# Latent attention on one core: full-row product of the query's high and the key's low part, query loads ahead of the key products, half of the key copies on GpSimd

## The chip, the cores and the metric

The kernel runs on one core of one Trainium2 chip. A core has five engines with a queue of instructions each: TensorE (PE, the matmuls; the profile shows its weight loads apart as PEld), VectorE (DVE), ScalarE (ACT), GpSimd (POOL) and SyncE (SP, which here issues nearly all DMAs). Each engine works through its queue in order, and semaphores tie the queues together. Matmul operands lie in SBUF with up to 128 rows (partitions), results go to PSUM. The metric is the device time of one execution in microseconds (us), lower is better.

## The reference: what is computed

The program is a two-layer trunk on 1024 tokens of width 1024, in float32: layer 0 mixes by a state-space scan and a convolution, layer 1 by a sparse attention and a latent attention, and each layer ends with an output product and a gated side input. The change lies in the latent attention of layer 1 alone:

```python
def mla_mixer(c_q, c_kv, k_rope, positions, q_norm, kv_norm, w_uq, w_ukv):
    q = (rms_norm(c_q, q_norm) @ w_uq).reshape(bsz, s_len, MLA_HEADS, MLA_NOPE + MLA_ROPE)     # 8 heads, 64 + 32
    kv = (rms_norm(c_kv, kv_norm) @ w_ukv).reshape(bsz, s_len, MLA_HEADS, MLA_NOPE + MLA_V)
    q = jnp.concatenate([q[..., :MLA_NOPE], rope(q[..., MLA_NOPE:], positions)], axis=-1)
    k_r = jnp.broadcast_to(rope(k_rope[:, :, None, :], positions), (bsz, s_len, MLA_HEADS, MLA_ROPE))
    k = jnp.concatenate([kv[..., :MLA_NOPE], k_r], axis=-1)
    v = kv[..., MLA_NOPE:]
    ...
    def one_block(i):                                                                          # 128 queries
        qb = lax.dynamic_slice_in_dim(q, t0, Q_BLOCK, axis=1)
        s = jnp.einsum('bqhd,bkhd->bhqk', qb, k).astype(f32) * scale
        mask = kpos[None] <= (t0 + jnp.arange(Q_BLOCK))[:, None]
        return jnp.einsum('bhqk,bkhd->bqhd', masked_softmax(s, mask), v)
```

## The kernel before

**Precision.** A product of two float32 matrices is made from split operands: a high part (rounded to the matmul's format) and a low part (the rest), as hi*hi + hi*lo + lo*hi. For a score, the 64 non-rotary features of one head are laid out so that one 128-row matmul carries two of these terms: query tile `QA` holds for each head the high part in one half of the rows and the low part in the other, key tile `KA` holds the key's high part in both halves. The third term, query high by key low, is a matmul of its own: it takes the 64 rows of `QA` with the high part, `QA[pr, h4]`, and 64 rows of `KB` with the key's low part (`KB` holds two heads, one in rows 0 to 63 and one in rows 64 to 127). The rotary features with all three terms are stacked on 96 rows (`QR`, `KR`).

**Order of the stage.** `layer1` runs the sparse attention `nsa`, then `mla_keys(0)`, then `mla`. `mla_keys(u)` makes the keys and values of four heads (u is 0 or 1): two products into PSUM (L1474), whose high part ACT writes to `kh` (L1476, in `parts` L107) and whose low part DVE writes to `KB` (L108); then eight DMAs from `kh` fill `KA` (L1479), four of which move 64 rows to other rows and four of which leave the rows as they are; then eight products of 128 tokens give the values `vm` (L1484, L1485). `mla` allots `qmslot`, makes POOL touch it behind `KA` (L1492), loads `KR` (L1493) and goes through 16 steps: u = 0 with eight blocks of 128 queries, then u = 1. A step loads `QA` and `QR` (L1501, L1502) into one of three places of `qmslot`, and the gate (L1504); then for each head the scores against n = 128 (i + 1) keys in pieces of at most 512 columns: `QA` by `KA` (L1518), on the last piece the causal mask as a bfloat16 matmul (L1263), `QA[pr]` by `KB` (L1521), `QR` by `KR` (L1522). DVE takes the row maximum (L1234), ACT the exponentials (L1237), DVE scales (L1246), PE transposes (L1258), ACT copies the transposes to SBUF (L1259), PE multiplies by the values (L1530), and `store_y` writes the result. Score tiles have two PSUM buffers of two banks. After step 3 `mla_keys(1)` runs.

**What sets the order.** Tiles and queues are planned by a scheduler that runs ahead of time: it keeps program order as priority, may put a ready instruction ahead of one that isn't, and fixes each engine's queue. `t16` tiles (16 KB a partition) share nine places; when `mla` begins, four of them hold the layer's output and five are given back by the sparse attention as its last reads end.

The sparse attention (`nsa`) has the same softmax and two score matmuls for each piece, L1333 with 128 rows and L1338 with 112.

Of the kernel before, what the change touches and what calls it, by code (L numbers as in the profile page):

```python
# [6 lines left out]
F32 = mybir.dt.float32  # L7
F32R = mybir.dt.float32r
# [14 lines left out]
class Trunk:  # L23
# [1441 lines left out]
    def mla_keys(self, u):  # L1465

        nc = self.nc
        if u == 0:
            self.KAm = []
            self.KBm, self.vm = self.t16([2, 2, 1024], F32R, name="KBm"), self.t16([2, 8, 256], name="vm")  # L1470
        KA, KB, vm = self.t16([4, 1024], F32R, name="KAm"), self.KBm[:, u], self.vm[:, u]
        Ck = [(self.Ck[:, 0], self.Ck[:, 1])]
        for q in range(2):
            ps = self.up(self.wk, 256 * u + 128 * q, Ck)  # L1474
            hi = self.t4((1024,), F32R, name="kh")
            self.parts(hi, KB[:, q], ps, nc.vector)  # L1476
            for b in range(2):
                for half in (0, 64):
                    nc.sync.dma_start(KA[half:half + 64, 2 * q + b].bitcast(F32), hi[64 * b:64 * b + 64].bitcast(F32))  # L1479
        vs = slice(512 + 256 * u, 768 + 256 * u)  # L1480
        for i in range(8):
            ts = slice(128 * i, 128 * i + 128)
# [4 lines left out]

    def mla(self):
        nc = self.nc
        Qs = self.t16([4, 2, 4, 128], F32R, name="qmslot")  # L1490
        KR = Qs[0:96, 3].rearrange("p a h t -> p (a h t)")
        self.after(KR[:, 0:1], self.KAm[0][0:96, 0, 0:1])  # L1492
        nc.sync.dma_start(KR.bitcast(F32), self.kr_dram.bitcast(F32))  # L1493
        for step in range(16):
            u, i = divmod(step, 8)
            ts = slice(128 * i, 128 * i + 128)
            nk, n = i + 1, 128 * (i + 1)
            hs = slice(4 * u, 4 * u + 4)
            KA, KB, vm = self.KAm[u], self.KBm[:, u], self.vm[:, u]
            QA, QR = Qs[:, step % 3, 0], Qs[0:96, step % 3, 1]  # L1500
            nc.sync.dma_start(QA.bitcast(F32), self.qm_dram[hs, :, ts].rearrange("h p t -> p h t").bitcast(F32))  # L1501
            nc.sync.dma_start(QR.bitcast(F32), self.qr_dram[hs, :, ts].rearrange("h p t -> p h t").bitcast(F32))  # L1502
# [5 lines left out]
            for s0 in range(0, 4, hg):  # L1508
                S = self.bank2().rearrange("p (h n) -> p h n", h=hg)
                for s_ in range(hg):  # L1510
                    b, q = divmod(s0 + s_, 2)
                    h4 = 2 * q + b
                    pr = slice(64 * b, 64 * b + 64)
                    for c in range(0, n, 512):
# [6 lines left out]
                        nc.tensor.matmul(o_, QA[pr, h4], KB[pr, q, ks], start=False, stop=False)  # L1521
# [16 lines left out]
    def layer1(self):  # L1538
# [30 lines left out]
        self.run(nsa)  # L1569
        self.mla_keys(0)  # L1570
# [70 lines left out]
```

## Time and profile before

| | |
|---|---|
| median of 3 runs | 1639.42 us (1637.12 to 1641.62) |
| profiled execution | 1643.63 us, of it span 1641.8 us |
| PE busy | 1522.7 us, 93% of the span, 8284 matmuls |
| DVE, ACT, POOL busy | 1004.4 (61%), 636.3 (39%), 360.4 us (22%) |
| chain that ended last | PE 72%, DVE 17%, DMA 3% |
| mean granted TensorE clock | 0.955 of full speed |
| latent attention in the span | from about 1211 us (first key product) to about 1428 us |

The profile is of one execution. A matmul's busy time is modelled with its drain, so neighbours overlap: what a matmul costs in a stream is the distance from its start to the start of the next one, which the text calls its pitch. The granted clock of 1.00 is 2.4 GHz, 0.50 is 1.2 GHz. "X <- Y" in a wait means that X sat idle until Y.

### The profile page before, as it was taken

The numbers are of one execution on the slowest core, as the hardware profiler recorded it, in microseconds if no ns is written. First come the engines' busy times: TensorE is split into PE (matmuls) and PEld (weight loads), VectorE is DVE, ScalarE is ACT, GpSimd is POOL, SyncE is SP. The second block draws the span as 40 slices with busy tenths as digits, with TensorE's granted clock in tenths as the row PEclk, the third lists the DMA queues.
The fourth block names the chain that finished last, engine by engine and source line by source line (L and its number), as shares of the span: only waits on it lengthen the run. The fifth ranks groups of instructions, "written<-read, shape, count | busy, mean of one in ns | idle before, by whom it ended". The sixth has DMA issues, their size and how long they took to land.

```text
span 1641.8 us, 22311 instructions
## 1 busy us (share of the span) xinstructions
PE 1522.7 (93%) x8284; PEld 1193.1 (73%) x8284; DVE 1004.4 (61%) x2248; ACT 636.3 (39%) x1297; POOL 360.4 (22%) x319
## 2 busy tenths in 40 slices
PE   4799899779998999799998979999999999999998
PEld 4697787667786888698876756666666676777787
DVE  6899999778435554751586246777744566444411
ACT  5332122166213333322342127777654565412210
POOL 4528633421225002312222200000000000132400
PEclk8899999889999999899999979999996999999999
DMA  8012453413424324242722264120043230422421
GB/s 244 14 52 79 139 180 111 146 52 129 157 78 142 128 87 135 82 143 85 180 90 90 77 193 125 54 67 22 27 98 85 66 92 25 143 95 94 151 87 68
DMA packets 140380, 168.65 MB, mean 103 GB/s; under 512 B 19432, under 2 KB 107232, under 8 KB 140272
## 3 DMA queue, kind: packets, MB, share of 16 engines
q1 hardware_dynamic: 135568, 155.82, 30.8%
q0 software_dynamic: 4544, 11.38, 2.3%
q8 instruction: 66, 1.08, 0.3%
q14 instruction: 42, 0.34, 0.1%
q10 hardware_dynamic: 160, 0.01, 0.0%
HBM read 112.10 MB, written 50.99 MB: 99 GB/s over the span
## 4 chain that ended last, share of the span: by engine, by line
PE 72%; DVE 17%; DMA 3%; ACT 2%; issue 2%; SPq 2%; POOL 1%; ACTq 0%; DVEq 0%; POOLq 0%
PE S L114 39%; PE tr L1258 7%; DVE conv L264 5%; PE o L1353 5%; PE tr L114 3%; PE o L1530 3%; PE S L1338 2%; PE S L1521 2%; PE S L1522 2%; PE S L1333 2%; PE S L1518 1%; PE tr L802 1%; PE S L1263 1%; SPq L1294 1%; PE tr L973 1%
## 5 line engine op out<-in xcount | busy, mean ns | idle before, releaser
L114 PE MATMUL S<-xT,wt 128*128 128x512 f32 x768 | 188.3, 401 | 4.3 <-DVE ext L249 4.3
L1234 DVE TENSOR_REDUCE nm<-S 128x1 f32<-128x640 f32 (+7 forms) x132 | 129.4, 981 | 101.8 <-PE S L1522 65.1
L114 PE MATMUL S<-X,wt 128*128 128x512 f32 x768 | 184.6, 396 | 5.8 <-ACT wt L107 2.3
L114 PE MATMUL S<-wo,Y 128*128 128x512 f32 x768 | 181.4, 395 | 5.0 <-DVE gb L688 3.6
L114 PE MATMUL S<-wg,hT 128*128 128x512 f32 x720 | 176.8, 403 | 9.5 <-ACT wg L107 4.0
L114 PEld LDWEIGHTS S<-xT,wt 128*128 128x128 f32 x768 | 144.9, 192 | 35.8 <-DVE ext L249 5.1
L114 PEld LDWEIGHTS S<-X,wt 128*128 128x128 f32 x768 | 143.1, 190 | 37.0 <-issue 4.0
L114 PEld LDWEIGHTS S<-wo,Y 128*128 128x128 f32 x768 | 143.8, 189 | 35.7 <-DVE gb L688 3.9
L114 PEld LDWEIGHTS S<-wg,hT 128*128 128x128 f32 x720 | 136.7, 193 | 42.2 <-ACT wg L107 7.3
L264 DVE SCALAR_TENSOR_TENSOR conv<-ext,conv 128x1024 f32<-128x1024 f32 x116 | 148.9, 1284 | 2.3
L108 POOL TENSOR_TENSOR wt<-raw,wt 128x1024 fp32r<-128x1024 f32 x34 | 82.8, 2451 | 115.9 <-ACT wt L107 115.8
L1237 ACT ACTIVATE pslot<-S,nm 128x640 f32<-128x640 f32 (+7 forms) x128 | 89.9, 709 | 25.6 <-DVE nm L1234 14.6
L1259 ACT COPY PT<-tr 128x512 f32<-128x512 f32 (+3 forms) x172 | 80.2, 492 | 46.5 <-PE tr L1258 42.3
L1258 PE MATMUL tr<-ident,pslot 128*128 128x128 f32 x528 | 84.7, 284 | 0.0
L1353 PE MATMUL o<-PT,vslot 128*64 128x256 f32 x528 | 84.5, 391 | 0.0
L1258 PEld LDWEIGHTS tr<-ident,pslot 128*128 128x128 f32 x528 | 58.7, 142 | 29.8 <-issue 20.8
L97 DVE TENSOR_SCALAR rs_v<-ss 128x1 f32<-128x1 f32 x32 | 4.9, 153 | 119.4 <-ACT lh L93 99.1
L1338 PE MATMUL S<-kst,qslot 112*128 112x512 f32 (+3 forms) x192 | 74.4, 400 | 0.0
L1333 PE MATMUL S<-kst,qslot 128*128 128x512 f32 (+3 forms) x192 | 70.3, 366 | 2.3 <-ACT pslot L1237 1.4
L787 POOL TENSOR_TENSOR lh<-lh 128x1024 f32<-128x1024 f32 x16 | 39.9, 2496 | 120.1 <-DVE lh L786 96.5
L852 DVE SCALAR_TENSOR_TENSOR ov<-ov,S 128x1024 f32<-128x1024 f32 (+1 forms) x17 | 19.7, 1157 | 73.3 <-issue 44.7
L93 ACT ACTIVATE lh<-S 128x1024 f32<-128x1024 f32 x16 | 16.4, 1028 | 123.3 <-issue 94.8
(433 smaller groups left out, 2858.8 us busy)
## 6 DMA issues: line engine op xcount, KB each, us to landing
h_dram<-lh POOLq DMA_DIRECT2D x16, 512.0 KB, 3.2
hr<-h_dram SPq DMA_DIRECT2D x14, 512.0 KB, 3.4
raw<-ev_w_in SPq DMA_DIRECT2D x16, 256.0 KB, 4.3
raw<-ev_w_in SPq DMA_DIRECT2D x8, 512.0 KB, 6.9
raw<-ev_w_out SPq DMA_DIRECT2D x8, 512.0 KB, 4.4
t<-ple_gate SPq DMA_DIRECT2D x8, 512.0 KB, 5.9
raw<-ple_gate SPq DMA_DIRECT2D x8, 512.0 KB, 6.3
lh<-x SPq DMA_DIRECT2D x8, 512.0 KB, 3.9
```

Source lines behind the costliest of these rows:

```text
L108: (eng or self.nc.gpsimd).tensor_tensor(lo, raw, hi, OP.subtract)
L114: self.nc.tensor.matmul(ps, l, r, start=n == 0, stop=n == len(seq) - 1)
L264: nc.vector.scalar_tensor_tensor(out=last if s == 30 else acc, in0=src, scalar=wc, in1=acc, op0=OP.mult, op1=OP.add)
L787: nc.gpsimd.tensor_tensor(hv, hv, xr, OP.add)
L1234: nc.vector.tensor_reduce(out=nm[:, 0:hg], in_=S[:, :, 0:n], op=OP.max, axis=AX.X, negate=True)
L1237: nc.scalar.activation(out=P[:, h, 0:n], in_=S[:, h, 0:n], func=AF.Exp, bias=nm[:, h:h + 1], accum_out=sm[:, h:h + 1])
L1258: nc.tensor.transpose(ps[:, c:c + 128], P[:, h, 128 * (k0 + k):128 * (k0 + k) + 128], self.ident)
L1259: nc.scalar.copy(PT[:, k0:k0 + n, s0:s0 + hg], ps[:, 0:128 * n * hg].rearrange("p (k h t) -> p k h t", h=hg, t=128))
L1333: nc.tensor.matmul(o_, QA[:, hd], KA[:, y, ks], start=True, stop=False)
L1338: nc.tensor.matmul(o_, qb[:, hd], KB[:, y, ks], start=False, stop=True)
L1353: nc.tensor.matmul(o[64 * y:64 * y + 64].rearrange("p g t -> p (g t)"), self.vsw[:, k0 + kt, 128 * br + 64 * y:128 * br + 64 * y + 64], PT ...
L1530: nc.tensor.matmul(o[64 * b:64 * b + 64, q], vm[:, kt, vs], PT[:, kt, 2 * b + q], start=(kt == 0), stop=(kt == nk - 1))
```

## The change

The query tile `qmslot` is allotted in a new function `mla_begin`, which `layer1` calls ahead of `mla_keys(0)`; there POOL zeroes two blocks of it and SP loads `KR` and the queries of steps 0 and 1. A step's queries now have two places in turn and not three, and a third query block `QB` takes, in two DMAs of 64 rows, the high parts alone, with zeros in the other 64 rows; the product with `KB` is then over all 128 rows. The loads of steps 2 to 15 stay at the head of their step. In `mla_keys`, the four copies to `KA` that keep their rows are made by POOL, the other four stay DMAs of SP. `KA` is allotted ahead of `KB` and `vm`.

```diff
--- before.py
+++ after.py
@@ -1465,10 +1465,11 @@
     def mla_keys(self, u):
 
         nc = self.nc
+        KA = self.t16([4, 1024], F32R, name="KAm")
         if u == 0:
             self.KAm = []
             self.KBm, self.vm = self.t16([2, 2, 1024], F32R, name="KBm"), self.t16([2, 8, 256], name="vm")
-        KA, KB, vm = self.t16([4, 1024], F32R, name="KAm"), self.KBm[:, u], self.vm[:, u]
+        KB, vm = self.KBm[:, u], self.vm[:, u]
         Ck = [(self.Ck[:, 0], self.Ck[:, 1])]
         for q in range(2):
             ps = self.up(self.wk, 256 * u + 128 * q, Ck)
@@ -1476,7 +1477,11 @@
             self.parts(hi, KB[:, q], ps, nc.vector)
             for b in range(2):
                 for half in (0, 64):
-                    nc.sync.dma_start(KA[half:half + 64, 2 * q + b].bitcast(F32), hi[64 * b:64 * b + 64].bitcast(F32))
+                    dst, src = KA[half:half + 64, 2 * q + b], hi[64 * b:64 * b + 64]
+                    if half == 64 * b:
+                        nc.gpsimd.tensor_copy(dst, src)
+                    else:
+                        nc.sync.dma_start(dst.bitcast(F32), src.bitcast(F32))
         vs = slice(512 + 256 * u, 768 + 256 * u)
         for i in range(8):
             ts = slice(128 * i, 128 * i + 128)
@@ -1485,21 +1490,42 @@
             nc.scalar.copy(vm[:, i], ps)
         self.KAm.append(KA)
 
+    def mla_begin(self):
+
+        nc = self.nc
+        Qs = self.Qm = self.t16([8, 4, 128], F32R, name="qmslot")
+        KR = self.KRm = Qs[0:96, 6:8].rearrange("p a h t -> p (a h t)")
+        for a in range(2):
+
+            nc.gpsimd.memset(Qs[:, 4 + a].bitcast(F32), 0.0)
+        self.mla_load(0)
+        nc.sync.dma_start(KR.bitcast(F32), self.kr_dram.bitcast(F32))
+        self.mla_load(1)
+
+    def mla_load(self, step):
+        nc, Qs = self.nc, self.Qm
+        u, i = divmod(step, 8)
+        ts, hs = slice(128 * i, 128 * i + 128), slice(4 * u, 4 * u + 4)
+        QA, QB, QR = Qs[:, step % 2], Qs[:, 4 + step % 2], Qs[0:96, 2 + step % 2]
+        nc.sync.dma_start(QA.bitcast(F32), self.qm_dram[hs, :, ts].rearrange("h p t -> p h t").bitcast(F32))
+        for b in range(2):
+            pr = slice(64 * b, 64 * b + 64)
+            nc.sync.dma_start(QB[pr, b:4:2].bitcast(F32),
+                              self.qm_dram[4 * u + b:4 * u + 4:2, pr, ts].rearrange("h p t -> p h t").bitcast(F32))
+        nc.sync.dma_start(QR.bitcast(F32), self.qr_dram[hs, :, ts].rearrange("h p t -> p h t").bitcast(F32))
+
     def mla(self):
         nc = self.nc
-        Qs = self.t16([4, 2, 4, 128], F32R, name="qmslot")
-        KR = Qs[0:96, 3].rearrange("p a h t -> p (a h t)")
-        self.after(KR[:, 0:1], self.KAm[0][0:96, 0, 0:1])
-        nc.sync.dma_start(KR.bitcast(F32), self.kr_dram.bitcast(F32))
+        Qs, KR = self.Qm, self.KRm
         for step in range(16):
             u, i = divmod(step, 8)
             ts = slice(128 * i, 128 * i + 128)
             nk, n = i + 1, 128 * (i + 1)
             hs = slice(4 * u, 4 * u + 4)
             KA, KB, vm = self.KAm[u], self.KBm[:, u], self.vm[:, u]
-            QA, QR = Qs[:, step % 3, 0], Qs[0:96, step % 3, 1]
-            nc.sync.dma_start(QA.bitcast(F32), self.qm_dram[hs, :, ts].rearrange("h p t -> p h t").bitcast(F32))
-            nc.sync.dma_start(QR.bitcast(F32), self.qr_dram[hs, :, ts].rearrange("h p t -> p h t").bitcast(F32))
+            QA, QB, QR = Qs[:, step % 2], Qs[:, 4 + step % 2], Qs[0:96, 2 + step % 2]
+            if step >= 2:
+                self.mla_load(step)
             sgm = self.t2([2, 128], name="sgm")
             nc.sync.dma_start(sgm, self.gm_dram[2 * u:2 * u + 2, :, ts].rearrange("g p t -> p g t"))
             hg = self.group_size(n)
@@ -1510,7 +1536,6 @@
                 for s_ in range(hg):
                     b, q = divmod(s0 + s_, 2)
                     h4 = 2 * q + b
-                    pr = slice(64 * b, 64 * b + 64)
                     for c in range(0, n, 512):
                         m = min(512, n - c)
                         ks = slice(c, c + m)
@@ -1518,7 +1543,7 @@
                         nc.tensor.matmul(o_, QA[:, h4], KA[:, h4, ks], start=True, stop=False)
                         if c + m == n:
                             self.add_mask(S[:, s_, n - 128:n], self.mask_diag)
-                        nc.tensor.matmul(o_, QA[pr, h4], KB[pr, q, ks], start=False, stop=False)
+                        nc.tensor.matmul(o_, QB[:, h4], KB[:, q, ks], start=False, stop=False)
                         nc.tensor.matmul(o_, QR[:, h4], KR[:, ks], start=False, stop=True)
                 P = self.t4(name="P").rearrange("p (h n) -> p h n", h=hg)
                 self.softmax_group(S, n, None, P)
@@ -1567,6 +1592,7 @@
         next(nsa)
         self.run(mq)
         self.run(nsa)
+        self.mla_begin()
         self.mla_keys(0)
         self.mla()
         self.Wo.append(self.out_weights(1, 1, self.w16))
```

## Rows read from the trace of the kernel before

**Rows 1.** Waits from 1262 to 1428 us: who waited for whom, us in total, times, longest.

```profile
DVE nm L1234 <- PE S L1522: 40.9, 35, 2.3
```

**Rows 2.** Busy time by stretch: us, engines busy (instructions), granted clock, DMA share, GB/s.

```profile
1180.00:1200.00 20.00, 20.00 (x143) 13.63 (x143) 15.46 (x33) 14.35 (x32) 0.00 (x0) 1.00 0.01 2
1228.00:1262.00 34.00, 34.00 (x115) 22.15 (x116) 11.64 (x30) 12.17 (x40) 0.00 (x0) 0.51 0.32 85
1262.00:1428.00 166.00, 166.00 (x1184) 116.14 (x1182) 95.49 (x203) 93.74 (x209) 8.03 (x6) 1.00 0.29 82
1510.00:1524.00 14.00, 9.96 (x37) 6.28 (x35) 8.69 (x16) 5.86 (x8) 6.09 (x5) 0.88 0.23 76
```

**Rows 3.** PE in order of time, one head with 768 keys: start, us, instruction.

```profile
1293.43 0.48 PE L1518 MATMUL S<-KAm,qmslot 128*128 128x512 f32 x1
1293.85 0.50 PE L1521 MATMUL S<-KBm,qmslot 64*128 64x512 f32 x1
1294.27 0.50 PE L1522 MATMUL S<-qmslot 96*128 96x512 f32 x1
1294.61 0.28 PE L1518 MATMUL S<-KAm,qmslot 128*128 128x256 f32 x1
1294.74 0.23 PE L1263 MATMUL S<-mbf 128*128 128x128 bf16 x1
1294.90 0.38 PE L1521 MATMUL S<-KBm,qmslot 64*128 64x256 f32 x1
1295.21 0.39 PE L1522 MATMUL S<-qmslot 96*128 96x256 f32 x1
1295.43 0.40 PE L1518 MATMUL S<-KAm,qmslot 128*128 128x512 f32 x1
```

**Rows 4.** PE in order of time, scores of the sparse attention, 512 columns.

```profile
1207.29 0.40 PE L1333 MATMUL S<-kst,qslot 128*128 128x512 f32 x1
1207.53 0.23 PE L1263 MATMUL S<-mbf 128*128 128x128 bf16 x1
1207.57 0.48 PE L1338 MATMUL S<-kst,qslot 112*128 112x512 f32 x1
1207.89 0.38 PE L1258 MATMUL tr<-ident,pslot 128*128 128x128 f32 x2
```

**Rows 5.** PE in order of time: 96-row product behind 128-row products of the values.

```profile
1277.75 0.63 PE L114 MATMUL tr<-Y,Y 128*128 128x256 f32 x3
1278.21 0.40 PE L1522 MATMUL S<-qmslot 96*128 96x512 f32 x1
1278.45 0.22 PE L1518 MATMUL S<-KAm,qmslot 128*128 128x128 f32 x1
```

**Rows 6.** PE in order of time, step 1: a last piece of 256 columns, half clock.

```profile
1235.33 0.41 PE L1518 MATMUL S<-KAm,qmslot 128*128 128x256 f32 x1
...
1236.70 0.41 PE L1518 MATMUL S<-KAm,qmslot 128*128 128x256 f32 x1
```

**Rows 7.** PE in order of time around the first score product.

```profile
1222.07 1.70 PE L114 MATMUL tr<-Y,Y 128*128 128x256 f32 x12
1227.83 0.44 PE L1518 MATMUL S<-KAm,qmslot 128*128 128x128 f32 x1 [4.06 <-DMA qmslot<-qm_dram]
```

**Rows 8.** SP's queue in order of time: DMA issues.

```profile
1213.84 7.45 SPq L1479 DMA_DIRECT2D KAm<-kh  x8
1222.12 0.95 SPq L1501 DMA_DIRECT2D qmslot<-qm_dram  x1
```

**Rows 9.** Time to landing of the DMAs that write KAm, then of those on qmslot.

```profile
DMA to landing us min/median/max: 3.0/4.8/5.8
...
DMA to landing us min/median/max: 2.6/3.1/5.6
```

**Rows 10.** Groups of POOL instructions by line and form: busy us, mean ns.

```profile
L1283 POOL MEMSET qslot<- 48x1024 f32 x2 | 1.9, 958 | 0.0
L1410 POOL COPY rtab<-sink 128x256 f32<-128x256 f32 x2 | 0.8, 400 | 0.0
```

## The prediction

> **What bounds the kernel now.** I read the stretches first, because the change touches one stage of 1641.8 us and the shares of the whole say nothing of it. From 1262 to 1428 us, the main part of the latent attention, PE is busy in all 166 us, while DVE has 95.5 and ACT 93.7 us of work [rows 2]. The list of waits says the same from the other side: DVE's largest wait is for the score product that ends a head, 40.9 us in 35 waits [rows 1]. So in this stage a microsecond off PE's stream is a microsecond off the end, until softmax work fills its engines. Second, the stretch from 1228 to 1262 us has PE just as full, with the granted clock at 0.51 (the lower level, 1.2 GHz, nearly throughout) [rows 2]. Third, I looked for what came just before: PE sat idle for 4.06 us until a query load had landed [rows 7]. Fourth, the order of PE in time at full clock, to read pitches (start to start): there the 64-row product shows what it costs [rows 3].
>
> **The full-row product.** In the piece of 512 columns without mask the pitches are 0.42 (L1518), 0.42 (L1521, 64 rows) and 0.34 us (L1522), together 1.18 [rows 3]. The sparse attention streams full-row products of 512 columns at 0.24, and pays only 0.04 from the mask to the product behind it and 0.32 for that product [rows 4]; here the mask costs 0.16 before L1521 may start [rows 3]. L1522 has 96 rows, so I checked that it is not dear by itself: behind 128-row products it starts 0.46 after the first of three, and the next product follows at 0.24 [rows 5]. So the 64 rows are what costs.
>
> Savings for each piece, at full clock. Without mask: L1521 0.42 to 0.24, L1522 0.34 to 0.24, and 0.09 of L1518's 0.42 (half of the excess over 0.24, since part of it is the entry behind the transposes): 0.37. With mask, at 256 columns: 0.16 to 0.04 ahead of L1521, 0.10 on L1521 (0.42 without a mask here against 0.32 behind the mask there, taken as the same at fewer columns), 0.10 on L1522: 0.32 [rows 3, 4, 5]. There are 16 steps of four heads, so 64 masked pieces; the 32 heads of the steps with more than 512 keys have a piece without mask too. Steps 0 to 3 (16 masked pieces) lie in the slow stretch and are counted there. The rest: 48 x 0.32 + 32 x 0.37 = 27.2 us off 166.
>
> Does the softmax let PE have it? 166 - 27 = 139 us would leave DVE at 69% and ACT at 67%; in the sparse attention DVE has 77% and ACT 72% of a stretch and PE is still never idle [rows 2]. But busy there includes stretched pitches, so I take off an eighth: 24 us, with 17 and 28 as bounds.
>
> A rule speaks against this edit. The 64-row product starts 0.16 us after a mask, the full-row one 0.04 [rows 3, 4]. The Trainium skill, "TensorE: Matmul & The Clock Gate", Part 3, says that a weight load overlaps matmuls in flight only when its row group differs. By it the 64-row slice would be the one that overlaps and a full-row one would not. The page "TensorEngine Tiling", Key Properties, says instead that a change of the tiling mode drains the engine; by that page the trace's order is as expected. The measurement decides for the second here; what the first would give is a rival below.
>
> **Query loads ahead of the key products.** Now SP issues eight key copies from 1213.84 on, 7.45 us in all, and the first query load stands behind them at 1222.12 [rows 8]; PE has its value products until 1223.77 (4.06 before 1227.83) and then waits [rows 7]. After the change KR and the queries of steps 0 and 1 (nine DMAs) are issued before the key copies, which needs the new place to be free: the trace does not show when that is. The sparse attention's last score product ends at about 1207.9 [rows 4]; if the place came free only then, nine issues of 0.5 to 0.95 us would reach past 1213.84 and push the key copies by up to 2.7 us. What is late next is `KA`. Four DMAs remain, at 7.45/8 = 0.93 us each, the last issued by about 1218, landing 4.8 (at most 5.8) later [rows 8, 9]: about 1223, just as PE gets there. So the wait falls from 4.06 to between 0 and 2; I take 4 us off. The two zero fills (nearest row 0.96 us for 48 x 1024) stand in a POOL that is idle at that time [rows 2, 10] and cost nothing; without that cover, 2 us.
>
> **Key copies on GpSimd.** A copy of 64 x 1024 has no row. The nearest copy, 128 x 256, takes 0.40 us, so four times that, 1.6, is the upper end, and the fill of 48 x 1024 at 0.96 the lower [rows 10]; I take 1.3. Two of them for each product end before the DMAs beside them land, so they are not last. For u = 1 they run in step 3 and are first read in step 8: hidden, with 8 us of POOL work in 166 [rows 2]. The gain is the shorter SP queue, counted above.
>
> **The clock.** If PE no longer idles for 4 us, I expect the clock to stay at 1.00 from 1228 on: the same short steps of u = 1 run within a stretch whose clock is 1.00 [rows 2]. A masked piece of 256 columns takes 1.37 us at the lower level [rows 6] and 0.82 at the upper [rows 3], a ratio of 0.60. The 34 us become 20.4; 16 pieces x 0.32 of the first edit take it to 15. ACT and DVE have 12.2 and 11.6 us of work in it [rows 2], so they don't bound it by volume, but the first softmaxes form a chain with little beside them, and the loads of steps 2 and 3 wait for their place. I add 5 (estimate: one load of four issues and a landing, 2 + 3.1 us [rows 8, 9]). So 34 becomes 20, 14 off. Bounds: 19 off without the chain; 5 off if the clock falls all the same (the pieces alone).
>
> **Two places for queries, not three, and four DMAs for a step, not two.** The load of step s now waits for the score products of step s - 2. Behind it on SP stand the gate's load and the next step's queries; who waits is PE. A load is about 2 us of issue and 3.1 to 5.6 until landed [rows 8, 9]; the cover is the PE work of step s - 1, 166/12 = 14 us in the mean, but only 2 to 4 us in steps 1 and 2 of either half. Exposed: steps 2, 3 (in the 5 above), 10 and 11, with step 7's rest as cover. I take 3 us on, bounds 0 and 8.
>
> **Sum.** 4 + 14 + 24 - 3 = 39 us off the profiled execution, 1643.6 to 1604.6. That execution is 4.2 above the median of the three runs, so against the median 1639.4 - 39 = 1600.
>
> **Rivals.**
> - The clock still falls at the start. For it: PE gaps well short of 4 us stand in a stretch whose clock is 0.88 (1510 to 1524 us) [rows 2]; the first softmax chain leaves such gaps. Against: denser products leave less idle time. The clock term shrinks from 14 to about 5, perhaps less when it recovers sooner: 1600 + 9 = 1609, to 1614 with a remaining wait of 2 and the longer loads.
> - The softmax becomes the bound. For it: DVE and ACT at 69 and 67% with chains across two score buffers. Against: the sparse attention [rows 2]. If PE gets only half of the 27 us: 24 - 13 = 11 less gain, 1611.
> - The full-row weight load does not overlap (the rule's case): three pitches near 0.42 in place of 0.24. Then the first edit gives nothing, in the slow stretch too, and 4 + 9 - 3 = 10 are left (14 less 5 there): 1629. Rows 4 speak against it.
> - Slower: starved loads. With two places, each of the steps 2 to 15 would have to wait for its queries. The other terms give 42 us, so it turns to a loss when the 14 loads cost over 3 us each, that is when a load takes over 14 + 3 = 17 us in the mean from the place coming free to landing, against 5 to 8 by the rows. At 20 us it would be 14 x 6 = 84 - 42 = 42 us slower, 1681.
> - It doesn't do what it says: the planner puts the query loads behind the key copies all the same. The 4 us and the clock's 9 are lost (14 less the 5 of the pieces), 1613.
>
> **How the numbers follow.** Forecast 0.60 (own range 1590 to 1608); clock falls 0.15; softmax 0.08; doesn't do what it says 0.05; no overlap 0.03; starved 0.04; 0.05 for a gain beyond the forecast's own range. All terms at their better ends give 4 + 19 + 28 = 51 off: 1588. All at their worse ends, 2 + 5 + 17 - 8 = 16 off: 1623. That range, 1588 to 1623, takes in the rivals but two and leaves out about 1 in 10. A measurement can tell 0.3%, 5 us: only the starved case and part of what lies beyond the worse ends reach there. Faster 0.92, same 0.04, slower 0.04.
>
> **What the next profile would show.** Right: L1521 with 128 rows, mask to L1521 at 0.04, L1521 and L1522 pitched near 0.24 for 512 columns; no PE wait over 2 us ahead of the first L1518; clock 1.00 from there; the first L1518 to the last L1530 in about 165 us where it now takes 200. Wrong: a clock of 0.50 behind the first score product, L1522 still at 0.34 or more, or PE waiting for DMAs on `qmslot` in steps 2, 3, 10 and 11 for over 3 us each.

## The result, and the profile after

The changed kernel takes 1603.05 us (median of four runs, 1601.52 to 1606.97) where the kernel before takes 1639.24: ratio 0.977, 95% interval 0.975 to 0.980, 36 us less. Its profiled execution is 1601.76 us with a span of 1599.7 us; that of before was 1643.63, so the two traces differ by 42 us and not by 36.

The first key product starts at 1208.8 us after the change and at 1211.1 us before it; these 2.3 us come from stages that the change doesn't touch, and in other kernels below this start lies anywhere up to 1217.3. So I compare one stretch, from the start of the first key product to the start of the last values product, and cut it where the scores of step 4 begin. All numbers called "stretch" are this:

| | stretch | to step 4 | from step 4 on | clock at 0.50 near the start |
|---|---|---|---|---|
| before | 215.4 | 58.1 | 157.3 | 34 us |
| after | 174.2 | 41.1 | 133.1 | 6.8 us |

It is 41.2 us shorter; the sum of the prediction was 39. First the scores of one head with 768 keys, PE in order of time (start, us, instruction), for comparison with [rows 3]:

```profile
1261.44 0.50 PE L1543 MATMUL S<-KAm,qmslot 128*128 128x512 f32 x1 [0.27 <-ACT P L1237]
1261.78 0.40 PE L1546 MATMUL S<-KBm,qmslot 128*128 128x512 f32 x1
1262.02 0.39 PE L1547 MATMUL S<-qmslot 96*128 96x512 f32 x1
1262.25 0.28 PE L1543 MATMUL S<-KAm,qmslot 128*128 128x256 f32 x1
1262.37 0.23 PE L1263 MATMUL S<-mbf 128*128 128x128 bf16 x1
1262.41 0.36 PE L1546 MATMUL S<-KBm,qmslot 128*128 128x256 f32 x1
1262.61 0.28 PE L1547 MATMUL S<-qmslot 96*128 96x256 f32 x1
1262.73 0.71 PE L1258 MATMUL tr<-ident,P 128*128 128x128 f32 x5
```

The piece of 512 columns goes from 1.18 to 0.81 us (0.34, 0.24, 0.23), the one of 256 with the mask from 0.82 to 0.48, and behind the mask the next product starts after 0.04. The 96-row product behind it is at full speed too.

Second, busy time by stretch of the changed kernel (us, then engines busy with instructions in the order PE, PEld, DVE, ACT, POOL, then the granted clock, the DMA share, GB/s), against [rows 2]:

```profile
1222.00:1228.00 6.00, 3.66 (x33) 3.33 (x31) 2.28 (x5) 3.37 (x15) 0.00 (x0) 0.97 0.28 82
1228.00:1234.00 6.00, 5.61 (x19) 4.13 (x20) 3.33 (x11) 2.96 (x11) 0.00 (x0) 0.50 0.47 128
1234.00:1240.00 6.00, 6.00 (x52) 4.47 (x51) 4.39 (x12) 3.24 (x11) 0.00 (x0) 0.96 0.41 120
1250.00:1383.00 133.00, 131.45 (x1116) 104.23 (x1115) 90.02 (x190) 86.69 (x198) 9.53 (x8) 1.00 0.35 98
```

The clock does fall again, but for 6.8 us. In the long stretch DVE has 68% and ACT 65% and PE is still nearly always busy: the softmax is not the bound. What DVE waits for says the same; waits of the changed kernel from 1250 to 1383 us (who waits for whom: us, times, longest), against [rows 1]:

```profile
DVE nm L1234 <- PE S L1547: 14.1, 23, 1.1
```

Third, what stands where the clock falls: PE in order of time at the end of step 1's scores, and the wait behind them.

```profile
1225.38 0.28 PE L1547 MATMUL S<-qmslot 96*128 96x256 f32 x1
1228.31 0.66 PE L1543 MATMUL S<-KAm,qmslot 128*128 128x384 f32 x1 [2.65 <-DVE P L1246]
```

In place of the wait of 4.06 us ahead of step 0 [rows 7] stands one of 2.65 ahead of step 2. SP's queue (issues in order of time) shows the other half of it:

```profile
1194.24 0.36 SPq L1510 DMA_DIRECT2D qmslot<-qm_dram  x1
...
1198.98 0.59 SPq L1515 DMA_DIRECT2D qmslot<-qr_dram  x1
1211.49 3.54 SPq L1484 DMA_DIRECT2D KAm<-kh  x4
...
1224.90 0.55 SPq L1510 DMA_DIRECT2D qmslot<-qm_dram  x1
```

The new place was free at 1194 us, so all nine first loads are over before the key copies begin; but the queries of step 2, which take step 0's place, are issued only at 1224.90, and this load landed at 1228.17 by the trace's record, 0.14 ahead of the product. GpSimd's copies are short:

```profile
1211.53 4.39 POOL L1482 CAST KAm<-kh 64x1024 fp32r<-64x1024 f32 x4 [16.25 <-ACT kh L107]
```

That is 1.04 us for each (median of eight), off PE's path as it seems. The experiments say otherwise.

### The profile page after: what moved, and what is told of

It reads as the page before. It is cut to its first block, busy times and chain, and to the rows that moved or that the text cites. A ratio compares the mean times of both kernels' runs of the same rounds, so it can differ in the third digit from the quotient of the medians.

```text
span 1599.7 us, 22369 instructions
## 1 busy us (share of the span) xinstructions
PE 1476.3 (92%) x8284; PEld 1175.7 (73%) x8284; DVE 1005.2 (63%) x2248; ACT 634.5 (40%) x1297; POOL 371.2 (23%) x328
## 4 chain that ended last, share of the span: by engine, by line
PE 67%; DVE 19%; issue 5%; DMA 3%; ACT 2%; SPq 2%; POOL 2%; ACTq 0%; POOLq 0%; DVEq 0%
PE S L114 36%; DVE conv L264 7%; PE tr L1258 7%; PE o L1353 5%; PE tr L114 3%; PE o L1555 3%; PE S L1338 2%; PE S L1333 2%; PE S L1546 1%; PE S L1543 1%; PE tr L802 1%; PE S L1547 1%; PE S L1263 1%; SPq L1294 1%; PE tr L973 1%
## 5 line engine op out<-in xcount | busy, mean ns | idle before, releaser
L114 PE MATMUL S<-xT,wt 128*128 128x512 f32 x768 | 188.1, 401 | 4.3 <-DVE ext L249 4.3
L114 PE MATMUL S<-X,wt 128*128 128x512 f32 x768 | 184.5, 396 | 5.8 <-ACT wt L107 2.3
L114 PE MATMUL S<-wg,hT 128*128 128x512 f32 x720 | 177.3, 403 | 10.6 <-ACT wg L107 4.5
L114 PE MATMUL S<-wo,Y 128*128 128x512 f32 x768 | 181.3, 394 | 4.5 <-DVE gb L688 3.1
L114 PEld LDWEIGHTS S<-xT,wt 128*128 128x128 f32 x768 | 144.8, 192 | 35.6 <-DVE ext L249 5.1
L114 PEld LDWEIGHTS S<-X,wt 128*128 128x128 f32 x768 | 143.0, 189 | 37.0 <-issue 4.0
L114 PEld LDWEIGHTS S<-wo,Y 128*128 128x128 f32 x768 | 143.9, 189 | 35.0 <-DVE gb L688 3.5
L114 PEld LDWEIGHTS S<-wg,hT 128*128 128x128 f32 x720 | 137.0, 194 | 43.6 <-ACT wg L107 7.8
L93 ACT ACTIVATE lh<-S 128x1024 f32<-128x1024 f32 x16 | 16.4, 1028 | 124.3 <-issue 94.9
```

Source lines behind the costliest of these rows:

```text
L114: self.nc.tensor.matmul(ps, l, r, start=n == 0, stop=n == len(seq) - 1)
```

## The experiments

The theory ahead of these runs: the full-row product gives nearly all of the later gain and part of the early one; the loads ahead of the keys and the clock give the rest; two places and GpSimd's copies cost next to nothing. What it says of GpSimd's copies fell.

**The 64-row product again.**

```diff
-  nc.tensor.matmul(o_, QB[:, h4], KB[:, q, ks], ...)
+  pr = slice(64 * b, 64 * b + 64)
+  nc.tensor.matmul(o_, QA[pr, h4], KB[pr, q, ks], ...)
```

> The changed kernel with one edit: the third term of a score is again the 64-row product of QA's high half by KB. The loads ahead of the key products, two places in turn, QB's loads and GpSimd's copies stay as they are. Theory (the full-row form gives about 27 us at full clock and about 5 more in the first steps): the pitches behind the 64-row product are again near 0.42/0.42/0.34 and the mask costs 0.16, so the run is 27 to 40 us longer than the changed kernel, about 1630 to 1641 us. Rival (the gain came from the loads and the clock; the row form is worth less than 10 us): at most 1612 us. On the clock the run also tells two things apart. If the low clock of the kernel before lasted 34 us because the products were sparse, the clock stays at 0.50 for 20 us and more here too, although the wait ahead of it is now only 2 to 3 us. If the length of the wait (4.06 us then) decided, the low stretch is under 10 us, as in the changed kernel (6.8 us).

Measured 1635.07 us, 0.996 of before (0.994 to 0.999): 32 us of the 36 are gone. PE's order of instructions is that of the changed kernel, one for one. Its head with 768 keys, as above:

```profile
1270.65 0.50 PE L1543 MATMUL S<-KAm,qmslot 128*128 128x512 f32 x1 [0.26 <-ACT P L1237]
1271.08 0.50 PE L1547 MATMUL S<-KBm,qmslot 64*128 64x512 f32 x1
1271.51 0.50 PE L1548 MATMUL S<-qmslot 96*128 96x512 f32 x1
1271.85 0.28 PE L1543 MATMUL S<-KAm,qmslot 128*128 128x256 f32 x1
1271.98 0.23 PE L1263 MATMUL S<-mbf 128*128 128x128 bf16 x1
1272.14 0.38 PE L1547 MATMUL S<-KBm,qmslot 64*128 64x256 f32 x1
```

The stretch is 207.1 us, 32.9 more than the changed kernel: 6.4 up to step 4, 26.5 behind it. The 64 rows cost what the prediction read from the kernel before (27.2). Summed from start to start over all scores from step 4 on, the first products take 20.6 us here and 17.6 in the changed kernel, the masks 7.6 and 2.0, the products with `KB` 30.0 and 18.4, the 96-row products 24.3 and 17.0. That is 27.5 us; a wait of 1.16 us for exponentials, which only the changed kernel has there, takes about 1 of them back. The clock lay between the two theories, at 0.50 for 13.6 us, so neither the row form alone nor the length of the wait alone decides how long it lasts. And it fell at 1227.7 us, a microsecond ahead of PE's wait (1228.67 to 1230.60): here the wait can't be what brought it down. PE in order of time; the product ahead of the wait already takes 0.58 us, where 256 columns take 0.39 at full clock [rows 3]:

```profile
1228.09 0.58 PE L1548 MATMUL S<-qmslot 96*128 96x256 f32 x1
1230.60 0.66 PE L1543 MATMUL S<-KAm,qmslot 128*128 128x384 f32 x1 [1.94 <-DMA qmslot<-qm_dram]
```

**Two places against three.** The run above, without QB's loads and zero fills, with three places of two blocks.

```diff
-  Qs = self.Qm = self.t16([8, 4, 128], F32R, name="qmslot")
+  Qs = self.Qm = self.t16([4, 2, 4, 128], F32R, name="qmslot")
-  QA, QB, QR = Qs[:, step % 2], ...
+  QA, QR = Qs[:, step % 3, 0], Qs[0:96, step % 3, 1]
...
```

> The changed kernel without its full-row product and without all that the product needs: the third term is the 64-row product, the queries have three places of two blocks again and two DMAs a step, QB and the zero fills are gone. What is left of the change are the loads ahead of the key products and GpSimd's four copies. Against the run with the 64-row product alone (stretch from the first key product to the last values product 207.1 us, 47.5 to the start of step 4 and 159.6 behind it) it shows what two places and four DMAs a step cost; the prediction put 3 us on that, bounds 0 and 8. Theory (they are covered nearly everywhere): a stretch of 204 to 207 us, about 1632 to 1636 us in all. Rival 1 (they cost as much as the prediction's worse end): 199 to 202 us. Rival 2 (the queue of PE is ordered worse without them): 208 us or more.

Measured 1635.60 us, stretch 207.1 (47.1 and 160.0) against 207.1 (47.5 and 159.6), PE's order the same. Two places and four DMAs a step cost nothing that shows in the sum, as the theory had it; the prediction had 3 us. It also shows what loads ahead and GpSimd's copies give without the full-row product: 0.998 of before (0.996 to 1.001) in time.

**One place**, to price a load that has less cover.

```diff
-  QA, QB, QR = Qs[:, step % 2], Qs[:, 4 + step % 2], Qs[0:96, 2 + step % 2]
+  QA, QB, QR = Qs[:, 0], Qs[:, 4], Qs[0:96, 2]
-  self.mla_load(1)
-  if step >= 2:
+  if step >= 1:
```

> The changed kernel with one edit: a step's queries have one place instead of two in turn, so the load of step s waits for the last score product of step s - 1 (step 1 is no longer loaded ahead). It prices a load that nothing covers. Theory (a load costs 2 us of issue and 3 us to landing, 5 us, partly covered by the transposes and value products that PE still has of the step before, 2 to 9 us in the longer steps): 15 loads expose 1 to 3 us each, 15 to 45 us in all, about 1620 to 1645 us, and the clock falls in several places. Rival 1 (nearly all of it is covered): under 10 us, 1613 us or less. Rival 2 (none is covered): 15 x 5 = 75 us, 1678 us, which is what the starved-loads case of the prediction needed.

Measured 1631.26 us, 0.995 of before (0.992 to 0.997); stretch 197.7, 23.5 more, 1.6 us for each of 15 loads. The list of PE's waits from 1217 to 1416 us names them:

```profile
PE S L1542 <- DMA qmslot<-qm_dram: 11.1, 9, 3.1
PE S L1546 <- DMA qmslot<-qr_dram: 5.3, 6, 3.3
```

These are 16.4 us; in addition the clock fell in four places, for 20.5 us together. So the rival of starved loads was far off even with a single place.

**Late loads.**

```diff
-        self.mla_begin()
         self.mla_keys(0)
+        self.mla_begin()
```

> The changed kernel with one edit: the query slot, its zero fills and the loads of KR and of steps 0 and 1 come behind the key products in the program, as before the change; full-row product, two places and GpSimd's copies stay. SP's queue is then four key copies and nine loads long when PE has ended the value products. Theory (the wait costs little by itself, and dense full-row products bring the clock back soon): PE waits 3 to 6 us ahead of the first score product, the clock falls to 0.50 and is back within 10 us, and the run is 4 to 9 us longer than the changed kernel, about 1607 to 1612 us. Rival (a wait of 4 us by itself brings the long low stretch of the kernel before, near 34 us): about 20 us longer, 1620 us or more.

Measured 1605.66 us, 0.978 of before (0.974 to 0.982), not to be told from the changed kernel in time; the stretch is 175.9, 1.7 us longer. PE in order of time, then the clock:

```profile
1227.32 0.35 PE L1543 MATMUL S<-KAm,qmslot 128*128 128x256 f32 x1 [1.98 <-DMA qmslot<-qm_dram]
```

```profile
1228.00:1238.00 10.00, 10.00 (x46) 8.87 (x45) 3.13 (x9) 3.59 (x16) 0.00 (x0) 0.50 0.42 119
1238.00:1244.00 6.00, 5.53 (x38) 3.90 (x36) 5.51 (x17) 4.24 (x16) 0.00 (x0) 0.98 0.45 128
```

A wait for queries is back, now ahead of step 1, and the clock falls for 10.2 us, not for 34. The theory had put more on it (a wait of 3 to 6 us, 4 to 9 us in all), the rival far more. But the wait came out at 1.98 us, so what a wait of 4 us does by itself isn't shown. With the full-row product the moved loads are worth 1.7 us of 41, and even these aren't theirs alone: up to step 4 PE's order is another one.

**Both undone**, the fourth corner of the square.

```diff
-  nc.tensor.matmul(o_, QB[:, h4], KB[:, q, ks], ...)
+  nc.tensor.matmul(o_, QA[pr, h4], KB[pr, q, ks], ...)
-        self.mla_begin()
         self.mla_keys(0)
+        self.mla_begin()
```

> The changed kernel with two edits: the third term is the 64-row product again, and the query slot and the first loads come behind the key products again. It is the fourth corner of a square: from the first key product to the last values product the changed kernel takes 174.2 us, with 64 rows alone 207.1, with late loads alone 175.9, the kernel before 215.4; the clock is at 0.50 for 6.8, 13.6, 10.2 and 34 us. What differs from the kernel before is then two places for three, QB's loads and GpSimd's copies. Theory (the low clock lasts long when 64-row products follow a long wait, so that the two effects do more together than one by one): 20 us and more at 0.50, a stretch of 211 to 216 us. Rival (they add up): 10 to 17 us at 0.50, a stretch of 208 to 210 us.

Measured 1651.11 us, 1.006 of before (1.004 to 1.008). The stretch is 219.1 (52.9 and 166.2), 10 us more than the sum of the two edits: 4.4 of them up to step 4, 5.9 behind it. Busy time of this kernel in its two stretches of low clock:

```profile
1231.00:1251.50 20.50, 18.42 (x68) 13.51 (x66) 5.38 (x16) 6.59 (x23) 0.00 (x0) 0.50 0.29 79
1330.00:1343.50 13.50, 13.50 (x66) 10.67 (x65) 4.80 (x15) 6.30 (x22) 0.00 (x0) 0.50 0.48 144
```

Up to step 4 the theory holds: with 64-row products the low stretch lasts twice as long (20.5 us against 10.2, and 13.6 against 6.8 with the loads ahead), and the two effects do more together. A wait of 2.1 us lies within the 20.5, though, and PE's order in the first steps is another one again, so the corners of the square differ by more than the two edits. The second stretch of low clock, which takes the run beyond both forecasts, no theory had: PE was busy right up to it and in all of it.

**All key copies as DMAs.**

```diff
-  if half == 64 * b:
-      nc.gpsimd.tensor_copy(dst, src)
-  else:
-      nc.sync.dma_start(dst.bitcast(F32), src.bitcast(F32))
+  nc.sync.dma_start(dst.bitcast(F32), src.bitcast(F32))
```

> The changed kernel with one edit: all eight key copies of each half are DMAs of SP again, none is made by GpSimd. Theory (GpSimd's share is worth next to nothing, since SP's queue is free of the query loads by then): SP needs 7.0 to 7.5 us for eight issues in place of 3.5 for four; the last is issued near 1219 and lands 4 to 5 us later, near 1223, while PE has its value products until about 1217. So the first score product on late keys comes up to 5 us later, but PE has the end of the sparse attention and single heads to put there: 0 to 4 us longer than the changed kernel, likely 2. Rival (the key copies decide the start, and the earlier start was what GpSimd bought): 5 to 10 us longer, with a wait of PE for KA of over 3 us and a longer stretch at 0.50.

Measured 1596.26 us, 0.972 of before (0.969 to 0.975), and the stretch is 166.6 us: 7.6 shorter than the changed kernel, 4.0 up to step 4 and 3.6 behind it. Neither theory had this sign. All runs lie below those of the changed kernel (at most 1597.30 us against at least 1601.52). PE in order of time: the first score, the last scores ahead of step 2 and the first of it:

```profile
1216.34 0.30 PE L1540 MATMUL S<-KAm,qmslot 128*128 128x128 f32 x1 [1.00 <-DMA KAm<-kh]
...
1224.94 0.28 PE L1540 MATMUL S<-KAm,qmslot 128*128 128x256 f32 x1
1225.06 0.23 PE L1263 MATMUL S<-mbf 128*128 128x128 bf16 x1
1225.10 0.60 PE L114 MATMUL tr<-Y,Y 128*128 128x256 f32 x3
1225.53 0.28 PE L1543 MATMUL S<-KBm,qmslot 128*128 128x256 f32 x1
...
1226.62 0.51 PE L114 MATMUL tr<-Y,Y 128*128 128x256 f32 x3
1227.64 0.41 PE L1540 MATMUL S<-KAm,qmslot 128*128 128x384 f32 x1 [0.51 <-DMA qmslot<-qm_dram]
...
1228.86 0.44 PE L1544 MATMUL S<-qmslot 96*128 96x384 f32 x1 [0.50 <-DMA qmslot<-qr_dram]
```

Value products (L114) stand between the scores. In the changed kernel they all stand ahead of the scores of the last six heads of steps 0 and 1, and PE has nothing left when it must wait for the first softmax. Here PE waits 1.00 us for `KA` at the start and 0.51 ahead of step 2, and the clock stays up, by busy time:

```profile
1222.00:1228.00 6.00, 5.49 (x46) 5.04 (x45) 2.73 (x5) 3.64 (x15) 0.00 (x0) 1.00 0.46 122
1228.00:1234.00 6.00, 5.50 (x39) 3.90 (x38) 5.07 (x19) 4.39 (x16) 0.00 (x0) 1.00 0.58 164
...
1246.00:1375.60 129.60, 129.60 (x1124) 104.53 (x1122) 90.37 (x191) 87.66 (x200) 8.04 (x6) 1.00 0.38 110
```

From step 2 to the end of the stage the planner's order of PE's instructions is here that of the kernel before; the changed kernel has another one. So the four GpSimd copies made the planner order PE's queue anew. That leaves two suspects, the order and the copying.

**Two GpSimd copies in place of four** tell them apart: PE's order is then, one for one, that of all DMAs.

```diff
-  if half == 64 * b:
+  if b == 1 and half == 64 * b:
       nc.gpsimd.tensor_copy(dst, src)
```

> The changed kernel with one edit: GpSimd makes only two of the eight key copies of each half (those of the second of each pair of heads), SP the other six. The planner's order of PE's instructions is then, instruction for instruction, the one of the kernel with all copies as DMAs, value products between the scores of the first steps included; the copies themselves still run on GpSimd. So it tells the order apart from the copying. Taken is the stretch from the first key product to the last values product: 174.2 us in the changed kernel, 166.6 with all copies as DMAs. Theory (the order of PE decides, GpSimd's copies are harmless): 166 to 168 us, clock at 1.00 throughout, about 1595 to 1598 us in all. Rival (GpSimd's copies cost the time, by holding up DVE or by arriving late): 169 us or more, about 1600 us, with DVE or PE waiting where the copies run.

Measured 1594.48 us, 0.972 of before (0.969 to 0.974), stretch 166.9 (37.2 and 129.6): with the order comes the whole gain, with two copies of each half on GpSimd or none. POOL in order of time (the second half's two are alike):

```profile
1213.48 1.04 POOL L1482 CAST KAm<-kh 64x1024 fp32r<-64x1024 f32 x1 [16.30 <-issue]
1215.68 1.04 POOL L1482 CAST KAm<-kh 64x1024 fp32r<-64x1024 f32 x1 [1.16 <-ACT kh L107]
```

**GpSimd in the first half only.**

```diff
-  if half == 64 * b:
+  if u == 0 and half == 64 * b:
```

> The changed kernel with one edit: GpSimd makes its four key copies for the first half only; the eight copies of the second half are DMAs of SP. PE's queue of the first steps is then as in the changed kernel (scores of steps 0 and 1 in one run, value products ahead of them), while the kernel with all copies as DMAs had value products between the scores. That kernel was 7 us shorter. Theory (its gain in the first steps came from that order, which closed the wait and kept the clock; its gain in the later steps, about 3.5 us, came from the order of steps 8 to 12): the start is as in the changed kernel, with a wait over 2 us and the clock at 0.50 for about 7 us, and the time lies at 1603 us, or up to 4 us below it if the later order follows the copies of the second half. Rival (GpSimd's copies themselves cost the time, by holding up DVE or SBUF in the second half): 3 us or more off, with the same order on PE.

Measured 1603.06 us, but from 1596.3 to 1606.6 in five runs, so the time settles nothing. The stretch is 169.9: 40.9 up to step 4, as the changed kernel, and 129.1 behind it, 4.1 less. Its wait ahead of step 2 stays:

```profile
1231.04 0.66 PE L1543 MATMUL S<-KAm,qmslot 128*128 128x384 f32 x1 [2.39 <-DVE sr L1244]
```

Up to step 4 PE's order is here that of the changed kernel, from late in step 4 on that of all DMAs. So the time follows the order in each part.

**The second half's keys behind step 1**, to fill the wait.

```diff
-            if step == 3:
+            if step == 1:
                 self.mla_keys(1)
```

> The changed kernel with one edit: the key products of the second half are called after step 1 and no longer after step 3. In PE's queue they then stand between step 1's scores and step 2's, where the changed kernel has the wait of 2.65 us behind which the clock fell. Theory (PE's idle time there is what brings the clock down, whatever the work that fills it): 12 key products of 512 columns, over 2 us, fill the wait; PE idles under 1 us, the clock stays at 1.00, and the run is 3 to 6 us shorter than the changed kernel, about 1597 to 1600 us. Rival (the fall is not tied to the idle time, or the keys only push the softmax chain and the same wait comes later): clock at 0.50 for 6 us or more again, time within 2 us of the changed kernel or longer.

Measured 1599.14 us, 0.975 of before (0.972 to 0.977), stretch 168.7 (38.3 and 130.4). The key products stand in the right place, but they wait too:

```profile
1231.03 2.90 PE L114 MATMUL S<-Y,Y 128*128 128x512 f32 x6 [1.91 <-ACT P L1237]
```

They write to a score buffer, and both are held until the exponentials of step 0 are done. So the wait is not filled, against the theory, though the time lies in its range; the clock is at 0.50 for 3.4 us, half as long. The run also shows a short rest (130.4) with all four GpSimd copies in both halves. From step 6 on its order of PE is that of all DMAs, and from there to the end both take 108.9 us, the changed kernel 111.9: 2.9 of the later 3.6 us are the order's and not the copies'. For the first steps no run has all four copies in that order; two of them in it give 37.2 up to step 4, none 37.1.

**The second half's values behind step 0**, work that comes too late for the wait.

```diff
...
-            if step == 3:
+            if step == 0:
+                self.mla_values(1)
+            elif step == 3:
                 self.mla_keys(1)
```

> The changed kernel with one edit: the value products of the second half (eight tokens blocks, 24 matmuls of 256 columns, about 3 us) are called after step 0, not behind the second half's key products after step 3. PE's queue gets them between the transposes of step 2 and after, not into the wait before step 2, since the program's order puts them behind step 1's scores only there. Theory (the wait ahead of step 2 stays, with the fall of the clock): same time as the changed kernel within 2 us, though 3 us of the work that ran at full clock in step 3 now runs at the lower one. Rival (any work near the wait helps to bring the clock back): 2 us or more off, with a stretch at 0.50 of under 5 us.

Measured 1605.28 us, 0.978 of before (0.976 to 0.981), stretch 174.2, wait 2.71 us, low clock 6.8 us: no gain, as the theory had it.

**Three places**, once on the changed kernel (steps 0 to 11) and once with all copies as DMAs (steps 0 to 7).

```diff
+  qc, rc = (self.praw.tile([128, 2, 4, 128], F32R, tag="raw", name=nm) for nm in ("qc", "rc"))
+  self.Qp = [(Qs[:, a], Qs[:, 4 + a], Qs[0:96, 2 + a]) for a in range(2)] + [(qc[:, 0], qc[:, 1], rc[0:96, 0])]
+  self.mla_load(2)
-  QA, QB, QR = Qs[:, step % 2], ...
+  QA, QB, QR = self.Qp[step % 3 if step < 12 else step % 2]
...
```

> The changed kernel with one edit: a third place for a step's queries, in two other tiles that are free in this stage, so that step 2's queries are also loaded ahead of the key products; steps 0 to 11 go through three places in turn, 12 to 15 through two. Theory A (PE's wait of 2.65 us before step 2, and with it the fall of the clock, is due to the late place for its queries): the wait shrinks to 1.8 us or less, the fall of the clock gets shorter or goes, and the run is 2 to 6 us shorter, about 1597 to 1601 us. Theory B (the wait is the first softmax chain, and the queries would only have landed at the same time): the wait stays at 2 us or more with the clock at 0.50 for 6 to 8 us, and the time stays within 1 us of the changed kernel.

> The kernel with all key copies as DMAs, with a third place for the queries of the first eight steps (step 2's are loaded ahead of the key products; from step 8 on two places in turn). PE's order is the same, instruction for instruction, as without the third place. In the kernel with all copies as DMAs PE waits 0.51 us for step 2's QA and 0.50 us for its QR. Theory (these two waits are the loads' alone): both go, and the stretch from the first key product to the last values product falls from 166.6 to 165.4 to 165.8 us; in all about 1 us, too little for the times to tell. Rival (the first softmaxes end no sooner, so the wait for a free score buffer takes their place): 166.4 us or more. A second rival: the longer queue of loads pushes the key copies or later loads, 168 us or more.

Measured 1602.64 us (0.976, 0.973 to 0.979) and stretch 174.3 for the first; 1595.52 us (0.973, 0.970 to 0.976) and 166.8 for the second. In both, the wait ahead of step 2 passes to the exponentials; first the first kernel, then the second, PE in order of time:

```profile
1229.45 0.69 PE L1545 MATMUL S<-KAm,qc 128*128 128x384 f32 x1 [1.91 <-ACT P L1237]
```

```profile
1232.51 0.44 PE L1542 MATMUL S<-KAm,qc 128*128 128x384 f32 x1 [0.49 <-ACT P L1237]
```

So of the 2.65 us of the changed kernel 0.74 are the late queries, and 1.91 are the softmax of step 0, which holds a score buffer. So theory B (but for its wait of 2 us or more) and the first rival hold: the load was not the last thing that was late. (The first kernel was 4.2 us ahead of the changed one at the start of step 12 and lost them within that step, with a wait of 2.25 us for exponentials and 3.4 us at 0.50. Step 12 is the first that goes through two places again; that this is the reason isn't shown.)

The kernel with two GpSimd copies, the one with none and the one with three places on top share one order of PE, and their times (1594.5, 1596.3, 1595.5) can't be told apart. All lie below both kernels of the case.

## Why the prediction was right, and where its steps were not

The time (1600, range 1588 to 1623) and the sign came true: 1603.05 us. Of the signs named ahead the pitches came, and about 165 us from the first score to the last values product (1217.76 to 1383.04 us); but so did one sign of being wrong, a clock of 0.50 behind the first scores. The steps one by one:

| step | predicted | shown |
|---|---|---|
| full-row product from step 4 on | 27.2, less an eighth: 24 | 26.5 (order as after), 27.8 (order as before, all DMAs) |
| wait for the first queries, and the clock, up to step 4 | 4 + 14 = 18 | 17.0, by another way |
| two places, four DMAs a step | 3 on | 0.0 |
| GpSimd's copies | hidden | 7.6 on, through PE's order |

- **Full-row product.** Right, and so was its reading from pitches: its rates give 2.9 us for the first products, 5.8 for the masks, 10.6 for the 64-row and 8.0 for the 96-row products; measured are 3.0, 5.6, 11.6 and 7.3. Of the eighth that I took off for the softmax, about 1 us shows in the changed kernel's order, and nothing with the order of the kernel before: there the stretch behind step 4 goes from 157.3 to 129.5 us, 27.8 off. That 24 came out for the changed kernel (157.3 to 133.1) is luck: 3.6 us went to the new order. 1.4 of them are the two waits of PE for exponentials (0.27 and 1.16 us). The rest lies in the main, by pitches, in transposes (1.2) and in value products (1.3): these pass into a score ten times in place of four, at 0.2 us a time, where one follows another at 0.06.
- **The rule.** In this kernel a full-row product streams behind another at 0.24 us for 512 columns, and the 64-row slice between full-row products is the one that takes 0.43. The weight loads (PEld) show where the overlap is; the load for the product with `KB`, first in the changed kernel, then with 64 rows:

```profile
1261.55 0.19 PEld L1546 LDWEIGHTS S<-KBm,qmslot 128*128 128x128 f32 x1
```

```profile
1271.08 0.18 PEld L1547 LDWEIGHTS S<-KBm,qmslot 64*128 64x128 f32 x1 [0.25 <-issue]
```

  The full-row load starts 0.23 us ahead of its product (1261.78), while the product before it runs; the 64-row load starts only with its own product (1271.08). The Trainium skill, "TensorE: Matmul & The Clock Gate", Part 3, has the overlap only for another row group, which would make it the other way round; the trace does not agree with it here. That a change of the tiling mode drains the engine (the Trainium skill, "TensorEngine Tiling (Array Packing)", Key Properties) agrees with the 64-row pitches. That rival, no overlap, falls.
- **The loads.** The place was free at 1194 us, better than I had assumed, and the planner did move all nine loads. But I named `KA` as the next to be late, and it wasn't (with all copies as DMAs PE does wait 1.00 us for it): the scores of steps 0 and 1 ran into the last of the sparse attention, and then the first softmax was late, with both score buffers held. I had this chain as 5 us within the clock's term and did not see that it makes a wait of its own, at which the clock fell. That the wait brought the clock down isn't shown: with the 64-row product, in the same order of PE, it fell ahead of the wait.
- **The clock.** The step "PE no longer idles, so the clock stays at 1.00" failed at its first half: PE idled for 2.65 us, and the clock fell for 6.8 us. (With all copies as DMAs the waits are 1.0, 0.5 and 0.5 us, and it does stay.) The rival that it falls all the same came true, but its price was wrong: I gave it 9 us, as if the low stretch would last as before, less the pieces. That the sum held up to step 4 has another cause: the low stretch was short. An estimate from rows: 1.4 us less of waiting, 27.3 us less at the lower level, of which 0.4 each is lost (the ratio of 0.60), and 16 pieces x 0.32, together 17.4, against 17.0 measured. By the square, the low stretches near the start are 34 us before, 20.5 with both edits undone, 13.6 and 10.2 with one undone, 6.8 with none: the full-row product halves them with the loads ahead or behind. The loads are worth 1.7 us of stretch with the full-row product and 12.0 without it. What lies between the 20.5 us and the 34 of before, no run shows.
- **The copies.** I asked whether they end in time, and they do. I did not ask what the planner makes of them. It is the one term that was missing, 7.6 us. That the sum came out right all the same is luck in this part: it hid behind two others that were too cautious, 3 for the places and 3 for the softmax.

The median fell by 36 and the traces differ by 42: the profiled execution of before lay 4 us above its median and that of after 1 us below, as the prediction's base had noted for before.

## What to carry to other kernels

A low-row matmul between full-row ones is priced from start to start, and together with its neighbours: padding 64 rows to 128 with zeros made three instructions faster, at the price of loads that were covered. Where a planner fixes the queues, an edit off the critical path can still reorder the path: compare the order of the bound engine's instructions before you call a moved copy free. And when a wait is removed at the start of a stage, look for what holds the buffers next; here an order of PE with value products between the first scores went with waits of 1.0 us and less and a clock that stayed up, while earlier loads only handed the wait to the softmax.

## What the runs showed of the hardware

- The clock can fall without idle time that the profile shows. With both edits undone it went to 0.50 at 1330.0 us, with PE busy without a break from 1316 us on. In the kernel with 64 rows and three places it fell at 1229.9 us, ahead of the wait; PE in order of time:

```profile
1229.72 0.48 PE L1540 MATMUL S<-KBm,qmslot 64*128 64x256 f32 x1
1230.13 0.58 PE L1541 MATMUL S<-qmslot 96*128 96x256 f32 x1
1232.00 0.69 PE L1536 MATMUL S<-KAm,qmslot 128*128 128x384 f32 x1 [1.29 <-ACT P L1237]
```

  The 96-row product of 256 columns takes 0.58 us, where it takes 0.39 at full clock [rows 3], and the wait comes only behind it. Short 64-row pieces precede both falls; yet the kernel with the 64-row product alone went through the pieces of the second half at 1.00. What decides a fall there, like the length of a low stretch, stays open.
- A GpSimd copy of 64 x 1024 takes 1.04 us, one of 128 x 256, with half as many elements on twice the partitions, 0.40 [rows 10]: four times the elements of a partition take 2.6 times as long.
